# Running decay sums of a Mamba layer: from broadcasting products on TensorE to a write to memory and four loads back

## The chip, the cores and the metric

The kernel runs on one core of a Trainium2 chip. The core has TensorE (PE: matrix products, with its weight loads as a track of their own, PEld), VectorE (DVE), ScalarE (ACT), GpSimd (POOL) and SyncE (SP, which here issues the transfers). Each engine works through its own row of instructions in order and waits on semaphores for the others. The on-chip memory has 128 partitions; products land in PSUM banks. The metric is the device time of one execution in microseconds (us), the median of several. A profiled execution gives busy times, waits and the clock that TensorE was granted (1.00 is full speed).

## The reference

Two layers of a decoder trunk run on 256 tokens of width 1024, in float32. The first is a hybrid attention mixer with a dense SwiGLU, the second a Mamba-2 mixer with a layer of eight experts. The change concerns the Mamba mixer alone. Cut to what matters:

```python
z, xbc, dt = split_cols(h @ w_in, SSM_SPLITS)
...                                                # causal convolution, silu
dt = softplus(dt + dt_bias); A = -exp(a_log)       # 32 heads
a = (dt * A)...
cum = jnp.cumsum(a, axis=-1)                       # running decay sums per head and chunk
seg = cum[..., :, None] - cum[..., None, :]
L = jnp.exp(jnp.where(causal, seg, -jnp.inf))
cb = jnp.einsum('bclgn,bcsgn->bgcls', Cc, Bc)
y_diag = jnp.einsum('bgcls,bgrcls,bcsgrp->bclgrp', cb, L, xdt)
decay_from_start = jnp.exp(cum)
...                                                # states across chunks, y_off
y = (y_diag + y_off) + d_skip[:, None] * x
y = y * silu(z)
y = rmsnorm(y, per group) * norm_w
return y @ w_out
```

There are 32 heads of width 64 in four groups of eight, a state of 128, and `w_in` has 5152 columns and `w_out` 2048 rows.

## The kernel before

Weights come from memory in blocks of 1 MB, which SyncE loads into a ring of buffers ("raw": nine during the Mamba stage, sixteen once that stage's pools are freed). For the products of full accuracy each half of a block is split: ScalarE casts it to its high part (`wh`, L252), VectorE subtracts that to get the low part (`wl`, L253), and four buffers of each are in turn. A product is then three (L267 high by high, L268 and L269 high by low both ways). The half of an input block is 24 such products of 256 columns.

The Mamba stage has these parts. First dt is projected and its softplus taken; a scan (L968) gives `cum`, the running decay sums, 32 heads on 32 partitions by 256 tokens, in chunks of 128. `s_proj` runs for each of the four groups through five input blocks (20 in all): the first three go through the convolution (L986 on ScalarE, three steps L988 on VectorE) into `xbc`, the last two give z, whose silu is `zs` (L1021), in a single buffer. `s_core` runs for each group (core 0 to 3 below): C times B (L1031, L1032), transposes of x (L1042) scaled into `xd` (L1044), and then four pairs of heads, j = 0 to 3. For a pair it needs the sums of two heads on all 128 partitions: `cums(j)` gets them with two products that pick a head's row (L1052, `pick` with `chl`, the sums split in high and low parts) into the PSUM bank "pb". ScalarE takes from there the four differences (L1066, relu into `seg`, two buffers), the decay from the start (L1069, exponential into `fo`) and the exponential of seg (L1070); VectorE multiplies by C times B (L1073, L1075); TensorE makes six products (L1080 to L1082, twelve instructions in the trace), and VectorE adds x (L1083) and multiplies by `zs` (L1085). A core ends with the norm of its group: the square of y (L1088), sums over partitions (L1091), `ms` (L1093), a product (L1096), a reciprocal square root on both engines (L338 to L342), and y scaled (L1101). `outs` splits y (L1115 cast, L1116 low part `yl`) and runs the output projection with 512-column products. When the stage is over, the expert weights follow to the end (L1313).

An order by hand, `SSM_ORDER`, writes the steps out (p: a step of `s_proj`, c: of `s_core`, m and t: of the next part's preparation; the output projection's are drained last). A scheduler then sets each engine's row from that, from what depends on what and from when it takes an engine to be free, so that a step taken away can shift others in the rows.

ScalarE's functions come in tables; a change from one set to another (silu, or exp with square root's) is an ACT_TABLE_LOAD.

Of the kernel before, what the change touches and what calls it, by code (L numbers as in the profile page):

```python
# [8 lines left out]
F32 = mybir.dt.float32  # L9
BF16 = mybir.dt.bfloat16  # L10
F32R = mybir.dt.float32r
# [5 lines left out]
D, T, KD = 1024, 256, 8  # L17
# [168 lines left out]
def trunk_kernel(ctx: ExitStack, tc: tile.TileContext, d: dict, out: bass.AP):  # L186
    nc = tc.nc
    V, S, G, PE = nc.vector, nc.scalar, nc.gpsimd, nc.tensor
# [8 lines left out]
    def pbank(tag):  # L197
        return ps_p.tile([128, 512], F32, name=tag, bufs=4 if tag == "pa" else 2)
# [12 lines left out]
    def P(n):  # L211
        s, w = _PC[n]
        return pc[:, s:s + w]

    def K(n):
        s, w = _CS[n]
        return cs[:, s:s + w]
# [6 lines left out]
    def ring(which):  # L224

        pools = raws if which == "raw" else hls
        i = turn[which] % sum(n for _, n in pools)
        turn[which] += 1
        for p, n in pools:
            if i < n:  # L230
                return p
            i -= n

    def load(ap):

        ap = ap.rearrange("p a b c -> p (a b c)") if len(ap.shape) == 4 else ap.rearrange("p a b -> p (a b)")
        r = ring("raw").tile([128, 2048], F32, name="raw")
        nc.sync.dma_start(r[:, :ap.shape[1]], ap)
        return r[:, :ap.shape[1]]
# [131 lines left out]
    def hpair():  # L371
        return (act_p.tile([128, KD, T], F32R, name="hh"), act_p.tile([128, KD, T], F32R, name="hl"))
# [31 lines left out]
    def norm_h(m, dg):  # L404
        A, B = mod_cols(m)
        h = hpair()
        norm_T(dg, lambda k, ps: split_act(h[0][:, k], h[1][:, k], ps, A[:, k:k + 1], B[:, k:k + 1], k % 2))
        return h
# [86 lines left out]
    h = hpair()  # L495
    with ExitStack() as hx:
# [245 lines left out]
        def all_values():  # L742
            for r in range(4):
                pos_.append(pbank("pa"))
                values(prs[r], pos_[r])
                yield

        def finish():
            for r in range(4):
                PE.matmul(pos_[r][:, :T], vcb[:, r], cpT, start=False, stop=True, skip_group_check=True)  # L750
                split_act(mb[0][:, r], mb[1][:, r], pos_[r][:, :T])
                yield
# [112 lines left out]
        def mods():  # L865
            for c in (4, 5):
                mod_load("hyb", 2 * c, 2 * c + 2)
                yield
            mod_gate("hyb", gate)
            yield  # L870
            for c in range(4):
                if c in (0, 3):
                    mod_load("dense", 2 * c, 2 * c + 2)
                else:
                    mod_sum(*mod_part("dense", c, hw.tile([128, 512], F32, name="at", bufs=1)))
                yield

        def consts():
# [6 lines left out]
                     V=all_values(), F=finish(), g=gla(), m=mods(), o=out_nsa())  # L885
# [19 lines left out]
    h = norm_h("dense", dgs)  # L905
# [46 lines left out]
    h = norm_h("ssm", dgs)  # L952
    with ExitStack() as sx:
        sy = sx.enter_context(tc.tile_pool(name="ssmy", bufs=3))
        sp = sx.enter_context(tc.tile_pool(name="ssm", bufs=1))
# [11 lines left out]
        cum = sw.tile([32, T], F32, name="fo")  # L967
        V.tensor_tensor_scan(cum, resets(sw, 32, T, 128, "seg"), dx_, 0.0, op0=OP.mult, op1=OP.add)  # L968

        chl = sp.tile([64, T], F32R, name="chl")  # L970
        S.copy(chl[:32], cum)
        V.tensor_sub(chl[32:], cum, chl[:32].bitcast(F32))
        pick = sp.tile([64, 32], F32R, name="pick")
        S.copy(pick, K("sel32")[:64])
        dtd = sw.tile([32, 128], F32, name="ms", bufs=1)
        act(dtd, cum[:, :128], AF.Exp, bias=cum[:, 127:128], scale=-1.0)
        V.tensor_mul(dtd, dtd, dtv[:, :128])
# [49 lines left out]
        def s_core(g):  # L1027
            xbc, zs = xz[g]
            bT, cT, xT = xbc[:, 0], xbc[:, 1], xbc[:, 2:]
            pcb = pbank("pc")  # L1030
            PE.matmul(pcb[:, :T], bT[:, :128], cT, start=True, stop=True)  # L1031
            PE.matmul(pcb[:, T:T + 128], bT[:, 128:], cT[:, 128:], start=True, stop=True)  # L1032
            cbm = sw.tile([128, 3, 128], F32, name="cbm", bufs=1)
            V.tensor_mul(cbm[:, 0], pcb[:, :128], tri)
            V.tensor_mul(cbm[:, 1], pcb[:, T:T + 128], tri)
            S.copy(cbm[:, 2], pcb[:, 128:T])
            xd = sw.tile([128, 3, 512], F32, name="xd", bufs=1)

            def x_tok(c):
                px = pbank("pc")  # L1040
                for j in range(4):
                    PE.transpose(px[:, j * 128:(j + 1) * 128], xT[:, j, c * 128:(c + 1) * 128], ident)  # L1042
                for o_, i in ((c, c),) + (((2, 4),) if c == 0 else ()):
                    V.tensor_mul(xd[:, o_].rearrange("p (h n) -> p h n", h=8),  # L1044
                                 px.rearrange("p (h n) -> p h n", h=8),
                                 tk[:, i, 8 * g:8 * g + 8, None].to_broadcast([128, 8, 64]))

            def cums(j):
                pcu = pbank("pb")
                for e in range(2):  # L1050
                    hh = 8 * g + 2 * j + e
                    PE.matmul(pcu[:, e * T:(e + 1) * T], pick[:, hh:hh + 1].to_broadcast([64, 128]), chl,  # L1052
                              start=True, stop=True)
                return pcu

            y = xT
            pcu = cums(0)
            x_tok(0)
            x_tok(1)
            yield  # L1060
            for j in range(4):
                h0 = 8 * g + 2 * j
                sg = sw.tile([128, 2, 2, 128], F32, name="seg")
                for e in range(2):
                    for c in range(2):
                        act(sg[:, e, c], pcu[:, e * T + c * 128:e * T + (c + 1) * 128], AF.Relu,  # L1066
                            bias=tk[:, 2 + c, h0 + e:h0 + e + 1], scale=-1.0)
                fo = sw.tile([128, 2, 128], F32, name="fo")
                act(fo, pcu.rearrange("p (e n) -> p e n", e=2)[:, :, 128:], AF.Exp)  # L1069
                act(sg, sg, AF.Exp, scale=-1.0)  # L1070
                if j < 3:
                    pcu = cums(j + 1)
                V.tensor_mul(sg.rearrange("p e c n -> p e (c n)"), sg.rearrange("p e c n -> p e (c n)"),  # L1073
                             cbm[:, 0:2].rearrange("p c n -> p (c n)")[:, None, :].to_broadcast([128, 2, 256]))
                V.tensor_mul(fo, fo, cbm[:, 2:3].to_broadcast([128, 2, 128]))  # L1075
                yield
                py = pbank("pc")
                for e in range(2):
                    o_, cc = slice(64 * e, 64 * e + 64), slice(128 * j + 64 * e, 128 * j + 64 * e + 64)
                    PE.matmul(py[o_, :128], xd[:, 0, cc], sg[:, e, 0], start=True, stop=True)  # L1080
                    PE.matmul(py[o_, 128:T], xd[:, 1, cc], sg[:, e, 1], start=True, stop=False)
                    PE.matmul(py[o_, 128:T], xd[:, 2, cc], fo[:, e], start=False, stop=True)  # L1082
                V.scalar_tensor_tensor(y[:, j], xT[:, j], P("dsk")[:, 4 * g + j:4 * g + j + 1], py[:, :T],  # L1083
                                       op0=OP.mult, op1=OP.add)
                V.tensor_mul(y[:, j], y[:, j], zs[:, j])  # L1085
                yield
            yt = sy.tile([128, 4, T], F32, name="y") if g < 3 else sw.tile([128, 4, T], F32, name="zs", bufs=1)
            act(yt, y, AF.Square)  # L1088
            pms = pbank("pc")
            for j in range(4):  # L1090
                PE.matmul(pms[32 * j:32 * j + 32, :T], K("ones")[:, :32], yt[:, j], start=True, stop=True)  # L1091
            ms = sw.tile([128, T], F32, name="ms", bufs=1)
            S.copy(ms, pms[:, :T])  # L1093
            yield
            pms = pbank("pc")
            PE.matmul(pms[:, :T], K("sel32")[:, :1].to_broadcast([128, 128]), ms, start=True, stop=True)  # L1096
            V.tensor_scalar(ms, pms[:, :T], 1.0 / 512, EPS, op0=OP.mult, op1=OP.add)
            ry = rsqrt_(ms, [128, T], sw, ("sq", "sq"))
            yield
            for j in range(4):  # L1100
                V.scalar_tensor_tensor(yt[:, j], y[:, j], P("sgn")[:, 4 * g + j:4 * g + j + 1], ry,  # L1101
                                       op0=OP.mult, op1=OP.mult)
            ys.append(yt)
            yield
# [84 lines left out]
    with ExitStack() as mx:  # L1189
# [342 lines left out]
        with tc.If(nmax > 0):  # L1532
# [3 lines left out]
            for h_ in range(2):  # L1536
                ps = pbank("pc")
                for q in range(4):
                    k = 4 * h_ + q
                    PE.matmul(ps[:, q * 128:(q + 1) * 128], macc["moe"][:, 16 + k:17 + k].to_broadcast([128, 128]),  # L1540
                              ident, start=True, stop=True)
                S.copy(gate[:, h_ * 512:(h_ + 1) * 512], ps)
            with tc.For_i(0, NE, 1) as e:
                for base in (0, 128):
# [23 lines left out]
                    for f0 in range(0, FE, 512):  # L1568
                        c, h_ = divmod(f0, 1024)
                        pgu = [pbank("pa") for _ in range(2)]  # L1570
                        for k in range(KD):
# [7 lines left out]
                            for u in range(2):  # L1579
                                PE.matmul(pgu[u].rearrange("p (j n) -> p j n", n=rk_.shape[3]), g2[:, k], rk_[:, u],  # L1580
                                          start=k == 0, stop=k == KD - 1)
# [11 lines left out]
                        for f in range(4):  # L1593
                            if f % 2 == 0:
                                r = load(d["e_dn"][bass.ds(e, 1), f0 // 256 + f // 2].rearrange("a p k n -> p a k n"))
                            for n in range(2):
                                PE.matmul(py[n], at[:, f * 128:(f + 1) * 128],
                                          r[:, (f % 2) * D + n * 512:(f % 2) * D + n * 512 + 512],
                                          start=f0 == 0 and f == 0, stop=f0 == FE - 512 and f == 3)
# [28 lines left out]
```

## Time and profile before

| what | value |
|---|---|
| median of 3 runs | 1454.12 us (1453.21 to 1457.64) |
| profiled execution | 1455.68 us, span 1453.7 us |
| busy: TensorE, VectorE, ScalarE | 1412.4, 562.8, 435.8 us |
| transfers | 493.66 MB, mean 340 GB/s |
| stages | hybrid to about 240 us, dense to 375, Mamba to 595, experts to the end |

Busy times count what an engine executes; a row of TensorE that is full says that it is not waiting, not that it is at its peak. In a timeline, the space from one start to the next is what an instruction costs in its row, and its duration can overlap the next one's.

### The profile page before, as it was taken

Reading aid. Unit: us, or ns where it says so; the run is one execution under the profiler, and the core shown is the slowest. Engines: PE = TensorE matmul, PEld = TensorE weight load, DVE = VectorE, ACT = ScalarE, POOL = GpSimd, SP = SyncE. Lnnn points to the kernel's source line nnn. Section 1 sums busy time; section 2 is a strip of 40 time slices with the busy share of each in tenths; the row PEclk is TensorE's granted clock in tenths of the full one; section 3 lists DMA queues with packets and bytes.
Section 4 is the critical chain, followed back from the end, with each engine's and each line's share of the span. In section 5 each row is a group of like instructions: output and inputs, shape, how many; then the busy total and the mean of one; then the engine's idle time right before and its main releaser. Section 6 shows DMA issues by size and latency. Waiting matters only on the chain.

```text
span 1453.7 us, 28564 instructions
## 1 busy us (share of the span) xinstructions
PE 1412.4 (97%) x12249; PEld 803.0 (55%) x12249; DVE 562.8 (39%) x1098; ACT 435.8 (30%) x854; POOL 5.3 (0%) x13
## 2 busy tenths in 40 slices
PE   6999999999999999999999999999999999999995
PEld 6866699999799987633433333333334333333331
DVE  7888588875678778510110111010100100100102
ACT  5577554444577685210100001000001000000001
POOL 0000000000000000000000000000000000000000
PEclk9999999999999999999999999999999999999998
DMA  9876778976544434799999999999999999999994
GB/s 382 351 271 251 297 295 334 375 300 241 232 146 154 165 117 144 286 397 363 350 413 420 420 420 420 417 421 420 420 420 419 420 421 420 420 419 420 420 420 163
DMA packets 68964, 493.66 MB, mean 340 GB/s; under 512 B 7648, under 2 KB 7904, under 8 KB 9568
## 3 DMA queue, kind: packets, MB, share of 16 engines
q1 hardware_dynamic: 68832, 491.77, 84.4%
q8 instruction: 98, 1.61, 0.4%
q14 instruction: 34, 0.28, 0.0%
HBM read 490.70 MB, written 1.05 MB: 338 GB/s over the span
## 4 chain that ended last, share of the span: by engine, by line
PE 93%; ACT 2%; DMA 2%; DVE 2%; issue 0%; SPq 0%; ACTq 0%; DVEq 0%
PE pa L1313 33%; PE pb L1313 16%; PE pa L267 7%; PE pa L268 7%; PE pa L269 7%; PE pb L268 3%; PE pb L269 3%; PE pb L267 3%; PE pc L1385 2%; PE pc L1347 1%; PE pc L1271 1%; DMA raw<-in_e_dn_dram 1%; ACT wh L252 1%; PE pb L702 1%; DMA raw<-in_hyb_mod_dram 1%; PE pa L732 1%
## 5 line engine op out<-in xcount | busy, mean ns | idle before, releaser
L1313 PE MATMUL pa<-raw,gx 128*32 128x512 f32 (+1 forms) x5120 | 506.4, 540 | 0.0
L1313 PEld LDWEIGHTS pa<-raw,gx 128*32 128x32 f32 x5120 | 167.2, 110 | 299.5 <-issue 261.3
L1313 PE MATMUL pb<-raw,at 128*32 128x512 f32 x2240 | 253.0, 594 | 2.2 <-DMA raw<-in_e_dn_dram 2.2
L1481 DVE TENSOR_TENSOR sg<-sg,pa 128x256 f32<-128x256 f32 (+1 forms) x80 | 31.0, 387 | 474.4 <-ACT sg L1480 472.7
L253 DVE TENSOR_TENSOR wl<-raw,wh 128x1024 fp32r<-128x1024 f32 (+1 forms) x155 | 185.4, 1204 | 57.2 <-ACT wh L252 57.0
L252 ACT CAST wh<-raw 128x1024 fp32r<-128x1024 f32 (+1 forms) x155 | 159.0, 1036 | 121.9 <-PE pb L268 53.0
L1313 PEld LDWEIGHTS pb<-raw,at 128*32 128x32 f32 x2240 | 70.5, 110 | 154.1 <-issue 144.8
L1480 ACT ACTIVATE sg<-pa 128x256 f32<-128x256 f32 (+1 forms) x80 | 28.5, 357 | 346.4 <-PE pa L1313 346.4
L267 PE MATMUL pa<-hh,wh 128*128 128x256 f32 (+1 forms) x392 | 112.4, 289 | 1.6 <-ACT wh L252 0.7
L268 PE MATMUL pa<-hl,wh 128*128 128x256 f32 (+1 forms) x392 | 111.4, 285 | 0.8 <-DVE hl L386 0.8
L269 PE MATMUL pa<-hh,wl 128*128 128x256 f32 (+1 forms) x392 | 111.3, 285 | 0.0
L267 PE MATMUL pb<-hh,wh 128*128 128x256 f32 (+1 forms) x360 | 101.8, 284 | 1.9 <-ACT hh L380 1.9
L268 PE MATMUL pb<-hl,wh 128*128 128x256 f32 (+1 forms) x360 | 102.3, 284 | 0.0
L269 PE MATMUL pb<-hh,wl 128*128 128x256 f32 (+1 forms) x360 | 102.2, 284 | 0.0
L1348 ACT COPY at<-pc 128x512 f32<-128x512 f32 (+2 forms) x32 | 17.4, 545 | 262.4 <-PE pb L1313 134.9
L281 DVE SCALAR_TENSOR_TENSOR junk<-raw,scb 128x1024 bf16<-128x1024 f32 x72 | 87.8, 1219 | 1.6 <-DMA raw<-in_hyb_mod_dram 1.0
L267 PEld LDWEIGHTS pa<-hh,wh 128*128 128x128 f32 (+1 forms) x392 | 73.8, 189 | 5.5 <-ACT wh L252 1.7
L268 PEld LDWEIGHTS pa<-hl,wh 128*128 128x128 f32 (+1 forms) x392 | 74.2, 189 | 2.1 <-DVE hl L386 0.9
L269 PEld LDWEIGHTS pa<-hh,wl 128*128 128x128 f32 (+1 forms) x392 | 74.1, 189 | 0.8 <-DVE gu L629 0.3
L267 PEld LDWEIGHTS pb<-hh,wh 128*128 128x128 f32 (+1 forms) x360 | 68.4, 190 | 2.9 <-ACT hh L380 2.1
L268 PEld LDWEIGHTS pb<-hl,wh 128*128 128x128 f32 (+1 forms) x360 | 68.6, 191 | 1.0 <-DVE hl L386 0.5
L269 PEld LDWEIGHTS pb<-hh,wl 128*128 128x128 f32 (+1 forms) x360 | 68.6, 191 | 0.3
(424 smaller groups left out, 1466.1 us busy)
## 6 DMA issues: line engine op xcount, KB each, us to landing
raw<-in_e_gu_dram SPq DMA_DIRECT2D x192, 1024.0 KB, 18.5
raw<-in_e_dn_dram SPq DMA_DIRECT2D x112, 1024.0 KB, 19.7
raw<-in_e_gl_dram SPq DMA_DIRECT2D x32, 1024.0 KB, 18.3
raw<-in_d_gu_dram SPq DMA_DIRECT2D x22, 1024.0 KB, 7.3
raw<-in_s_in_dram SPq DMA_DIRECT2D x20, 1024.0 KB, 4.8
raw<-in_hyb_mod_dram SPq DMA_DIRECT2D x12, 1024.0 KB, 9.6
raw<-in_ssm_mod_dram SPq DMA_DIRECT2D x12, 1024.0 KB, 7.1
raw<-in_d_dn_dram SPq DMA_DIRECT2D x11, 1024.0 KB, 7.9
```

The lines of the kernel that those rows point to most:

```text
L252: hi_last[0] = S.copy(hi[:, :n], r)
L253: lo_last[0] = V.tensor_sub(lo[:, :n], r, hi[:, :n].bitcast(F32))
L267: PE.matmul(ps, a[0], b[0], start=start, stop=False, **kw)
L268: PE.matmul(ps, a[0], b[1], start=False, stop=False, **kw)
L269: return PE.matmul(ps, a[1], b[0], start=False, stop=stop, **kw)
L281: V.scalar_tensor_tensor(jk, r[:, q * D:(q + 1) * D], 1.0, scb, op0=OP.mult, op1=OP.mult, accum_out=macc[m][:, 2 * j + q:2 * j + q + 1])
L702: PE.matmul(pss[g], qbT[g * 64:(g + 1) * 64, r, q * 128:(q + 1) * 128], kT[g * 64:(g + 1) * 64, :, :n], start=True, stop=True)
L1313: up_last[0] = PE.matmul(ps[32 * j:32 * j + 32, :rhs.shape[1]], lhs, rhs, start=start, stop=stop)
L1348: (V.tensor_copy if i else S.copy)(at[:, i:i + n].rearrange("p a n -> p (a n)"), pt_[:, :n * 128])
L1385: PE.matmul(pso[b], at_place[e, q][:, h, b], p[:, q], start=i == 0, stop=i == 2 * n - 1)
L1480: last = act(sg[:, r, :w], pg[r][:, :w], AF.Silu)
L1481: V.tensor_mul(sg[:, r, :w], sg[:, r, :w], pg[r][:, w:2 * w])
```

## The change

The sums in high and low parts and the table that picks a head are gone, and so are the 32 products. Instead ScalarE's queue writes `cum` (32 x 256 floats, 32 KB) to a buffer in memory, and at the start of each core SyncE's queue loads the eight heads of its group, 2048 floats in one row, to all 128 partitions at once: one block of 1 MB in the ring of weight buffers. The relus and exponentials read their two heads from there. The order by hand is as it was.

```diff
--- before.py
+++ after.py
@@ -967,11 +967,8 @@
         cum = sw.tile([32, T], F32, name="fo")
         V.tensor_tensor_scan(cum, resets(sw, 32, T, 128, "seg"), dx_, 0.0, op0=OP.mult, op1=OP.add)
 
-        chl = sp.tile([64, T], F32R, name="chl")
-        S.copy(chl[:32], cum)
-        V.tensor_sub(chl[32:], cum, chl[:32].bitcast(F32))
-        pick = sp.tile([64, 32], F32R, name="pick")
-        S.copy(pick, K("sel32")[:64])
+        dr = sx.enter_context(tc.tile_pool(name="dr", bufs=1, space=bass.MemoryType.DRAM)).tile([32, T], F32, name="dr")
+        S.dma_start(dr, cum)
         dtd = sw.tile([32, 128], F32, name="ms", bufs=1)
         act(dtd, cum[:, :128], AF.Exp, bias=cum[:, 127:128], scale=-1.0)
         V.tensor_mul(dtd, dtd, dtv[:, :128])
@@ -1045,13 +1042,10 @@
                                  px.rearrange("p (h n) -> p h n", h=8),
                                  tk[:, i, 8 * g:8 * g + 8, None].to_broadcast([128, 8, 64]))
 
+            cb = load(dr[8 * g:8 * g + 8].rearrange("h n -> (h n)")[None, :].to_broadcast([128, 8 * T])[:, None, :])
+
             def cums(j):
-                pcu = pbank("pb")
-                for e in range(2):
-                    hh = 8 * g + 2 * j + e
-                    PE.matmul(pcu[:, e * T:(e + 1) * T], pick[:, hh:hh + 1].to_broadcast([64, 128]), chl,
-                              start=True, stop=True)
-                return pcu
+                return cb[:, 2 * j * T:2 * (j + 1) * T]
 
             y = xT
             pcu = cums(0)
```

Line numbers of the kernel after are 3 lower from L974 on, and 6 lower behind L1052 (L1080 is L1074, L1115 is L1109).

The rows of the engines move with it. On TensorE, before, at the last product of the input projection (L269 with `hh`, `wl`) and what stands behind it, unit j = 3 of core 2, a pair of sums for core 3 and the first products of the output projection (`wh`, `hh`):

```order
L268 MATMUL pa<-hl,wh 128x256
L269 MATMUL pa<-hh,wl 128x256
L1080 MATMUL pc<-seg,xd 64x128
L1081 MATMUL pc<-seg,xd 64x128
L1082 MATMUL pc<-fo,xd 64x128
L1080 MATMUL pc<-seg,xd 64x128
L1081 MATMUL pc<-seg,xd 64x128
L1082 MATMUL pc<-fo,xd 64x128
L1052 MATMUL pb<-chl,pick 128x256 x2
L267 MATMUL pa<-wh,hh 128x512
```

Now the same place holds core 2's units j = 2 and 3 (the end of the second is shown), then the four sums of squares of its norm, the norm, C times B and the transposes of core 3, and only then the output projection:

```order
L1076 MATMUL pc<-fo,xd 64x128
L1074 MATMUL pc<-seg,xd 64x128
L1075 MATMUL pc<-seg,xd 64x128
L1076 MATMUL pc<-fo,xd 64x128
L1085 MATMUL pc<-y,cs 32x256 x4
L1090 MATMUL pc<-ms,cs 128x256
L1028 MATMUL pc<-xbc 128x256
L1029 MATMUL pc<-xbc 128x128
L1039 MATMUL pc<-cs,xbc 128x128 x4
L267 MATMUL pa<-wh,hh 128x512
L268 MATMUL pa<-wl,hh 128x512
```

What moved: no product of the output projection stands between the last input block and core 2's norm any more.

On ScalarE, before, in the same place, the cast of y of core 0 (L1115) and the relus of a pair of core 3 stand ahead of the silu of z (L1021) and the square of core 2's y (L1088):

```order
L252 CAST wh<-raw 128x1024 x2
L1115 CAST hh<-y 128x1024
L1066 ACTIVATE seg<-pb,tk 128x128 x4
L1069 ACTIVATE fo<-pb 128x256
L1070 ACTIVATE seg<-seg 128x512
L252 CAST wh<-raw 128x1024
L1021 ACT_TABLE_LOAD
L1021 ACTIVATE zs<-pa 128x512 x2
L348 ACT_TABLE_LOAD
L1088 ACTIVATE y<-xbc 128x1024
L1115 CAST hh<-y 128x1024
L1093 COPY ms<-pc 128x256
```

Now (the four relus of core 3's first pair stand right ahead):

```order
L1063 ACT_TABLE_LOAD
L1063 ACTIVATE fo<-raw 128x256
L1018 ACT_TABLE_LOAD
L1018 ACTIVATE zs<-pa 128x512 x2
L348 ACT_TABLE_LOAD
L1082 ACTIVATE y<-xbc 128x1024
L1064 ACTIVATE seg<-seg 128x512
L1060 ACTIVATE seg<-raw,tk 128x128 x4
L1087 COPY ms<-pc 128x256
L1063 ACTIVATE fo<-raw 128x256
L1064 ACTIVATE seg<-seg 128x512
L1109 CAST hh<-y 128x1024
```

What moved: the cast of y of core 0 stands behind the silu, the square and the copy of `ms`, and there is a table load on each side of fo.

On VectorE, before, from the norm of core 1 (L1101) to the next split of weights, with the convolution of core 3's input:

```order
L1101 SCALAR_TENSOR_TENSOR y<-xbc,pc,sq 128x256 x4
L1044 TENSOR_TENSOR xd<-pc,tk 128x512
L988 SCALAR_TENSOR_TENSOR xbc<-pa,pc,xbc 128x255
L1073 TENSOR_TENSOR seg<-seg,cbm 128x512
L988 SCALAR_TENSOR_TENSOR xbc<-pa,pc,xbc 128x254
L1075 TENSOR_TENSOR fo<-fo,cbm 128x256
L988 SCALAR_TENSOR_TENSOR xbc<-pa,pc,xbc 128x253
L988 SCALAR_TENSOR_TENSOR xbc<-pa,pc,xbc 128x255
L253 TENSOR_TENSOR wl<-raw,wh 128x1024
```

Now the end of the same stretch, from the second fo behind that norm to the next split:

```order
L1069 TENSOR_TENSOR fo<-fo,cbm 128x256
L985 SCALAR_TENSOR_TENSOR xbc<-pa,pc,xbc 128x255 x2
L985 SCALAR_TENSOR_TENSOR xbc<-pa,pc,xbc 128x254 x2
L985 SCALAR_TENSOR_TENSOR xbc<-pa,pc,xbc 128x253 x2
L1077 SCALAR_TENSOR_TENSOR xbc<-xbc,pc 128x256
L985 SCALAR_TENSOR_TENSOR xbc<-pa,pc,xbc 128x255 x3
L985 SCALAR_TENSOR_TENSOR xbc<-pa,pc,xbc 128x254 x2
L985 SCALAR_TENSOR_TENSOR xbc<-pa,pc,xbc 128x253 x2
L985 SCALAR_TENSOR_TENSOR xbc<-pa,pc,xbc 128x254
L1079 TENSOR_TENSOR xbc<-xbc,zs 128x256
L985 SCALAR_TENSOR_TENSOR xbc<-pa,pc,xbc 128x253
L253 TENSOR_TENSOR wl<-raw,wh 128x1024
```

What moved: the split that stood behind four convolution steps stands behind fifteen.

## Rows read from the trace of the kernel before

**Rows 1.** Three stretches: length, busy us (instructions) of each engine, PEclk, DMA, GB/s:

```profile
400.00:595.00 195.00, 194.45 (x1438) 174.16 (x1436) 150.42 (x266) 134.43 (x231) 0.00 (x0) 1.00 0.40 141
640.00:740.00 100.00, 100.00 (x1075) 37.70 (x1071) 9.42 (x30) 10.85 (x28) 0.00 (x0) 1.00 0.96 367
740.00:1425.00 685.00, 676.66 (x6595) 241.00 (x6587) 73.27 (x162) 59.70 (x139) 0.00 (x0) 1.00 1.01 420
```

**Rows 2.** Timeline of TensorE: start, duration, engine, line, operation, tiles, shape, count, [idle before]:

```profile
403.15 0.36 PE L267 MATMUL pa<-hh,wh 128*128 128x256 f32 x1 [0.25 <-DVE xbc L988]
...
478.68 0.28 PE L268 MATMUL pa<-hl,wh 128*128 128x256 f32 x1
478.80 0.28 PE L269 MATMUL pa<-hh,wl 128*128 128x256 f32 x1
479.01 0.50 PE L1052 MATMUL pb<-chl,pick 64*128 64x256 f32 x2
479.44 0.43 PE L1080 MATMUL pc<-seg,xd 128*64 128x128 f32 x2
...
480.51 0.50 PE L1052 MATMUL pb<-chl,pick 64*128 64x256 f32 x2
```

**Rows 3.** Landing time of the broadcast load of a 4 KB row, line 944:

```profile
DMA to landing us min/median/max: 4.6/4.6/4.6
```

**Rows 4.** The page's DMA issues: tiles, queue, count, KB each, us to landing:

```profile
raw<-in_e_gu_dram SPq DMA_DIRECT2D x192, 1024.0 KB, 18.5
```

**Rows 5.** Timeline of VectorE, after the scan and ahead of the convolutions:

```profile
396.41 0.68 DVE L968 TENSOR_TENSOR_SCAN fo<-seg,sq 32x256 f32<-32x256 bf16 x1
...
503.42 1.21 DVE L253 TENSOR_TENSOR wl<-raw,wh 128x1024 fp32r<-128x1024 f32 x1
...
505.62 0.68 DVE L1044 TENSOR_TENSOR xd<-pc,tk 128x512 f32<-128x512 f32 x1
506.22 0.41 DVE L342 SCALAR_TENSOR_TENSOR sq<-sq 128x256 f32<-128x256 f32 x1
...
507.16 1.66 DVE L1101 SCALAR_TENSOR_TENSOR y<-xbc,pc,sq 128x256 f32<-128x256 f32 x4
...
510.45 0.47 DVE L988 SCALAR_TENSOR_TENSOR xbc<-pa,pc,xbc 128x254 f32<-128x254 f32 x1
510.84 0.41 DVE L1075 TENSOR_TENSOR fo<-fo,cbm 128x256 f32<-128x256 f32 x1
...
511.95 1.21 DVE L253 TENSOR_TENSOR wl<-raw,wh 128x1024 fp32r<-128x1024 f32 x1
```

**Rows 6.** Timeline of ScalarE, at the first sums and at the tail of core 2:

```profile
404.52 1.17 ACT L1066 ACTIVATE seg<-pb,tk 128x128 f32<-128x128 f32 x4
...
406.31 1.10 ACT L252 CAST wh<-raw 128x1024 fp32r<-128x1024 f32 x1
...
527.64 1.14 ACT L1066 ACTIVATE seg<-pb,tk 128x128 f32<-128x128 f32 x4
528.80 1.28 ACT L1069 ACT_TABLE_LOAD   x1
530.09 0.39 ACT L1069 ACTIVATE fo<-pb 128x256 f32<-128x256 f32 x1
530.37 0.62 ACT L1070 ACTIVATE seg<-seg 128x512 f32<-128x512 f32 x1
...
533.88 1.04 ACT L1115 CAST hh<-y 128x1024 fp32r<-128x1024 f32 x1 [1.01 <-PE pa L269]
...
539.01 1.09 ACT L1021 ACTIVATE zs<-pa 128x512 f32<-128x512 f32 x2
...
543.31 0.36 ACT L1093 COPY ms<-pc 128x256 f32<-128x256 f32 x1
```

**Rows 7.** Stretches of the first layer in which the granted clock fell:

```profile
82.00:87.00 5.00, 3.03 (x12) 1.33 (x12) 3.98 (x14) 4.89 (x14) 0.00 (x0) 1.00 1.02 429
87.00:91.00 4.00, 4.00 (x35) 1.59 (x34) 4.00 (x8) 2.51 (x8) 0.00 (x0) 0.57 1.07 397
```

## The prediction

> **What bounds the kernel now.** I read the stretches first: between 400 and 595 us, the Mamba stage around the change, TensorE is busy 194.45 of 195 us at the full granted clock, while VectorE is busy 150, ScalarE 134 and the DMA engines 0.40 of the time [rows 1]. The stage is TensorE's, and what is taken out of its row, or put into it as idle time, is what moves. The same view tells how a shift there reaches the end: from 640 to 740 us TensorE is still busy the whole time and the transfers run at 367 GB/s, because they wait for it; from 740 on they run at 420 GB/s with nothing left over [rows 1]. In both stretches the expert weights come through a ring of buffers that is full, so a shift of the stage's end shifts the kernel's end one for one, in either direction.
>
> Then the timeline of TensorE: a pair of L1052 products takes 0.43 us, from its start at 479.01 to the next product at 479.44, and the twelve L1080 to L1082 instructions of one head pair (a unit, below) take 1.07 us, to 480.51 [rows 2]. Plain products of 256 columns start 0.12 us apart (478.68, 478.80) [rows 2].
>
> **What the change takes away.** There are 16 pairs: 16 x 0.43 = 6.9 us of TensorE's row. At 403.15, right behind the first pairs, TensorE waits 0.25 us for a convolution result [rows 2]; there a removed pair only makes the wait longer, so I count 6.6 us. The cast and subtraction that split the decay sums (L971, L972) and the cast of the selection table (L974) lie beside TensorE's work, and I count nothing for them.
>
> **What it adds on the transfers.** One write of 32 KB from ScalarE's queue and four loads of 1 MB in SyncE's queue, each in a slot of the nine-slot ring. 4 MB in a stage whose DMA engines are busy 0.40 of the time costs nothing by itself, and of the nine slots one is held by the sums at a time. The trace has no write like it and no load that repeats one row of 8 KB over 128 partitions. The nearest row is a load that repeats a 4 KB row, 512 KB, in 4.6 us [rows 3]; the far one is a block of the expert weights in the crowded stretch, 18.5 us [rows 4]. With 4.6 us each for write and load, from the scan's end at 397.1 (396.41 + 0.68) [rows 5], the first sums are there at 406.3. ScalarE wants them at 404.52, and the cast behind them stood at 406.31 [rows 6]; so that cast comes about 2 us later. Three halves of weights cast ahead, of 24 products each, are 3 x 24 x 0.12 = 8.6 us of work for TensorE, which covers that. Below nothing it can't go, since nobody waited for the sums before. I take 0, by the nearest row; the far one is a rival below. What is queued behind that load on SyncE (further blocks of the input projection) has its cover in the blocks already in the ring. For the write only a page has a price: the Trainium skill (DMA: Bandwidth & Descriptors, Latency and other measured facts) speaks of about 2 us of fixed cost, most of it the receipt from memory; as an estimate by it the first sums would land at 403.7 us, and the sum below stays as it is. No run here shows that yet.
>
> **What it moves.** With fewer products in the row, all of the input projection comes ahead of the second half of core 2 (the third group of heads), and the first products of the output projection come behind that core's norm. Two places pay.
>
> First, VectorE ahead of the last blocks of the input projection. In the row of before, 9.7 us lie from the start of one low-part split (503.42) to the end of the next (511.95 + 1.21) [rows 5], with four convolution steps between them, and TensorE doesn't wait. In the changed row the stretch between two such splits holds three xd products and two of seg at 0.60 each, three steps of the square root, two of fo and two of y at 0.41, the four of y's norm in 1.66 and fifteen convolution steps at 0.39 [rows 5]: 3.0 + 2.9 + 1.7 + 5.9 = 13.5 us, and the two splits at its ends 2.4, together 15.9. TensorE's row holds in the same time 73 products of the input projection, 73 x 0.12 = 8.8, two units, 2.1, and eight transposes, at most 1.0: 11.9 us. Then it wants the split that stands behind the convolution steps. Ends: 0 (if TensorE comes late to that place itself, as it did before) and 4.0, the whole difference; durations overlap a little in such a row, so I take 3.5.
>
> Second, the tail of core 2. In TensorE's row behind the last product of the input projection stand only units j = 2 and 3 (2.1 us), four sums of squares, the norm, C times B and the transposes, and then the output projection. In the row of before its products stand between them, and the cast of y that they need is done early (533.88) [rows 6]. In the changed row of ScalarE that cast stands behind the whole tail. The chain there, from the last product: 0.9 for unit 2, whose seg buffer the next relus reuse; four relus 1.14; a table load 1.28; fo 0.28; a table load 1.28; the two zs 1.09; a table load 1.28; the square of y, as wide as the cast, 1.04 [rows 6]. That is 8.3 us, of which TensorE fills 2.1: 6.2 idle. Then the exponential (0.62), four relus (1.14) and the copy of ms (0.36) [rows 6], 2.1 us, of which the four sums fill 4 x 0.12: 1.6 idle. Then fo, exponential and cast, 0.28 + 0.62 + 1.04 = 1.9, against seven products (0.9) and a VectorE step (0.41) between them: 0.6 idle. Last the low part of y, 1.2 by the split of the same width, against three products of 512 columns (0.7): 0.5 idle. Together 8.9 us. Lower end 2.7 (only the last three waits stay, if relus and tables come early), upper end 10.
>
> **TensorE's clock.** From 82 to 87 us TensorE was busy 3.03 of 5 us at the full clock, and in the next 4 us, with work all the time, the granted clock was 0.57, so mostly the lower of its two levels, 1.2 GHz [rows 7]. That lost 4 x 0.43 = 1.7 us. Both places make stretches with more idle time than that. Ends 0 and 3.4; I take 0.7, since the low clock can also fall on time that is idle anyway. The Trainium skill (TensorE: Matmul & The Clock Gate, Why this matters for your kernels) has a rule that speaks against this change: no idle gaps between bursts of matmuls, or the array goes back to 1.2 GHz; the trace agrees, with its 0.57. By that rule the tail would pay its 1.7 us for certain, and the kernel would take 1461.6 us.
>
> **Sum.** -6.6 + 0 + 3.5 + 8.9 + 0.7 = +6.5 us. On the profiled execution, 1455.68 us (its span of 1453.7 and 2 us around it), that makes 1462.2; this execution stands 1.6 above the median of the runs, 1454.12, and on the median the forecast is 1460.6 us.
>
> **Rivals.**
> Faster: the whole 6.6 us reach the end, 1447.5 us. The mechanism: at the tail of core 2 ScalarE runs ahead, and the relus and tables are done while TensorE is still in its last block. For it: ScalarE is busy only 134 of 195 us [rows 1]. Against it: those relus need the seg buffer that unit 2 still reads, and that unit stands behind the last block. It decides from the point where both places idle less than 6.6 us together.
> About the same: the first place costs nothing and the tail's 8.9 us come without a fall of the clock: +2.3, 1456.4 us. For it: before, TensorE bore 9.7 us between two splits without waiting [rows 5]. Against it: 15.9 is half as much again.
> Slower still: both places at their upper ends, each with a fall of the clock: -6.6 + 4.0 + 8.9 + 3.4 = +9.7, 1463.8 us. For it: the 0.57 [rows 7].
> The transfers don't do what they should: 128 reads of the same 8 KB are as slow as a block in the crowded stretch, 18.5 us [rows 4]. Then the first sums come at 397.1 + 4.6 + 18.5 = 420.2, ScalarE stands with its casts behind them, TensorE runs out of split weights at about 415 and gets the next at 424: 9 us more than the forecast, 1470 us. Against it: this stretch is not crowded.
>
> **How the numbers follow.** Forecast 0.45, about the same 0.30, faster 0.12, slower still 0.08, slow transfers 0.05. 0.3% of the median is 4.4 us, about what a measurement of this kernel can tell from no change. Of the forecast's 0.45 some 0.06 fall under 4.4 us (the first place at 1 us or below). So slower 0.39 + 0.08 + 0.05 = 0.52, within 0.3% 0.36, faster 0.12. The likeliest case alone spans 1456.5 to 1464; the range reaches down into the upper part of the faster case and up past the third rival, but not to the fourth: 1449 to 1466.
>
> **What would show it.** Right: no L1052 and some 6.6 us less work in TensorE's row; waits of TensorE for wl (L253) or xbc ahead of the last input blocks of 1 to 4 us; behind the last input product, waits for the square of y, for ms and for the cast of y that sum to about 9 us; a granted clock under 1 there; the first expert products 5 to 7 us later. Wrong: TensorE's waits in the Mamba stage staying under 4 us (then the same or faster), or a wait of ScalarE of more than 5 us for a load of the sums (then the fourth rival).

## The result and the profile after

The changed kernel takes 1468.27 us (median of 5, 1462.43 to 1472.46), the kernel before 1457.64 us (median of 5, 1453.21 to 1459.69): a ratio of 1.0077, 95% interval 1.0056 to 1.0098, some 11 us slower. The forecast was 1460.6 us, a range of 1449 to 1466, and 6.5 us slower. So the direction and both places were right, the size was short, and the time lies above the range. The profiled execution of after is the fastest of its five (1462.43 us, span 1460.5).

The three stretches of [rows 1], in the same view of after:

```profile
400.00:595.00 195.00, 183.27 (x1350) 166.91 (x1351) 144.31 (x249) 134.84 (x224) 0.00 (x0) 0.96 0.51 183
640.00:740.00 100.00, 100.00 (x1075) 37.72 (x1071) 8.58 (x28) 10.11 (x26) 0.00 (x0) 1.00 0.95 367
740.00:1425.00 685.00, 677.06 (x6577) 240.33 (x6570) 73.57 (x162) 58.74 (x138) 0.00 (x0) 1.00 1.01 420
```

The Mamba stage is no longer full: TensorE stands still for 11.7 of 195 us and has 0.96 of its clock, where it had 0.6 us and 1.00. The experts' stretches are unchanged. What TensorE waits for from 372 to 612 us (line waited at, releaser, us in total, times, longest): before has two in the stage,

```profile
PE pa L267 <- ACT wh L252: 0.3, 1, 0.3
PE pa L267 <- DVE xbc L988: 0.3, 1, 0.3
```

and after has

```profile
PE pc L1085 <- ACT y L1082: 7.0, 1, 7.0
PE pa L267 <- DVE xbc L985: 2.8, 2, 1.6
PE pa L269 <- DVE wl L253: 2.1, 1, 2.1
PE pc L1090 <- ACT ms L1087: 0.9, 1, 0.9
```

These are the two places of the forecast, and one more wait of 1.2 us for xbc at 400, where before waited 0.25 [rows 2]. The timeline of TensorE shows them, and what comes behind the first and the longest:

```profile
397.20 1.84 PE L321 MATMUL pc<-cs,part 128*128 128x1 f32 x16
400.24 0.36 PE L267 MATMUL pa<-hh,wh 128*128 128x256 f32 x1 [1.20 <-DVE xbc L985]
...
402.10 0.41 PE L268 MATMUL pa<-hl,wh 128*128 128x256 f32 x1
402.31 0.41 PE L269 MATMUL pa<-hh,wl 128*128 128x256 f32 x1
...
514.92 0.35 PE L267 MATMUL pa<-hh,wh 128*128 128x256 f32 x1 [1.59 <-DVE xbc L985]
...
517.47 0.47 PE L269 MATMUL pa<-hh,wl 128*128 128x256 f32 x1 [2.07 <-DVE wl L253]
...
538.95 1.08 PE L1085 MATMUL pc<-y,cs 128*32 128x256 f32 x8 [6.96 <-ACT y L1082]
540.89 1.22 PE L1090 MATMUL pc<-ms,cs 128*128 128x256 f32 x2 [0.86 <-ACT ms L1087]
541.90 1.06 PE L1028 MATMUL pc<-xbc 128*128 128x256 f32 x2
542.76 0.63 PE L1029 MATMUL pc<-xbc 128*128 128x128 f32 x2
543.18 1.06 PE L1039 MATMUL pc<-cs,xbc 128*128 128x128 f32 x4
543.90 0.78 PE L267 MATMUL pa<-wh,hh 128*128 128x512 f32 x1
```

From 540.89 to 543.90 nothing waits, and yet a few small products take 3.0 us. In the timeline of before the same norm and C times B take 1.00 us, from 543.97 to the next product at 544.97; here they take 2.29 (540.89 to 543.18):

```profile
543.97 0.59 PE L1096 MATMUL pc<-ms,cs 128*128 128x256 f32 x2
...
544.97 0.48 PE L268 MATMUL pa<-wl,hh 128*128 128x512 f32 x1
```

The granted clock says why. Stretches of after in the form of [rows 7]:

```profile
402.00:404.00 2.00, 2.00 (x11) 2.00 (x11) 2.00 (x5) 1.74 (x6) 0.00 (x0) 0.50 1.01 422
518.00:520.00 2.00, 2.00 (x11) 2.00 (x11) 2.00 (x5) 0.00 (x0) 0.00 (x0) 0.50 0.84 352
534.00:538.00 4.00, 0.00 (x0) 0.00 (x0) 0.17 (x1) 3.97 (x6) 0.00 (x0) 0.59 0.74 256
538.00:546.00 8.00, 6.19 (x26) 4.54 (x27) 3.73 (x8) 6.55 (x14) 0.00 (x0) 0.57 0.00 0
```

The clock falls to 1.2 GHz in three places: at 402, behind sixteen products of one column each and the wait of 1.2 us; at 518, behind 1.6 and 2.1 us; and in the long wait itself, from about 534.7 to 545, and in some 5 us of that TensorE works. The transfers, against [rows 3, 4] (the page's form, a median for the four loads):

```profile
raw<-dr SPq DMA_DIRECT2D x4, 1024.0 KB, 4.7
...
dr<-fo ACTq DMA_DIRECT2D x1, 32.0 KB, 1.5
```

They cost as little as assumed: 4.7 us for a broadcast load (the median of four; the second took 10.3), 1.5 us for the write. That is less than the 2 us that the Trainium skill speaks of (DMA: Bandwidth & Descriptors, Latency and other measured facts). ScalarE waits for none of the loads; its first relus on them start right behind its casts:

```profile
398.79 2.96 ACT L252 CAST wh<-raw 128x1024 fp32r<-128x1024 f32 x3
401.62 1.29 ACT L1060 ACTIVATE seg<-raw,tk 128x128 f32<-128x128 f32 x4
```

To compare executions I use the length of the Mamba stage from the scan to the first expert product. The run's other part varies by falls of the clock in the first layer, which the change doesn't touch: before lost 5.1 us of full clock there (18 to 24, 86 to 92 and 100 to 106 us) and after's profiled execution none; its scan starts 2.9 us earlier. Before goes from 396.41 [rows 5] to

```profile
604.89 0.64 PE L1313 MATMUL pa<-raw,gx 128*32 128x512 f32 x4
```

which is 208.5 us; after (VectorE's and TensorE's timelines) takes 217.4 us, 8.9 more:

```profile
393.48 0.68 DVE L968 TENSOR_TENSOR_SCAN fo<-seg,sq 32x256 f32<-32x256 bf16 x1
...
610.86 0.64 PE L1307 MATMUL pa<-raw,gx 128*32 128x512 f32 x4
```

### The profile page after: what moved, and what is told of

Its sections match the earlier page's. It is cut to its first block, busy times and chain, and to the rows that moved or that the text cites. A ratio compares the mean times of both kernels' runs of the same rounds, so it can differ in the third digit from the quotient of the medians.

```text
span 1460.5 us, 28513 instructions
## 1 busy us (share of the span) xinstructions
PE 1406.8 (96%) x12217; PEld 800.6 (55%) x12217; DVE 562.6 (39%) x1097; ACT 440.6 (30%) x854; POOL 5.3 (0%) x13
## 4 chain that ended last, share of the span: by engine, by line
PE 87%; DMA 5%; DVE 3%; ACT 3%; issue 1%; SPq 0%; ACTq 0%
PE pa L1307 31%; PE pb L1307 15%; PE pa L267 7%; PE pa L268 7%; PE pa L269 7%; PE pb L268 3%; PE pb L269 3%; PE pb L267 3%; DMA raw<-in_e_dn_dram 2%; PE pc L1379 2%; PE pc L1265 1%; DMA raw<-in_e_gl_dram 1%; DMA raw<-in_e_gu_dram 1%; PE pc L1341 1%; PE pb L400 1%
## 5 line engine op out<-in xcount | busy, mean ns | idle before, releaser
L269 PE MATMUL pa<-hh,wl 128*128 128x256 f32 (+1 forms) x392 | 112.3, 288 | 2.1 <-DVE wl L253 2.1
L269 PE MATMUL pb<-hh,wl 128*128 128x256 f32 (+1 forms) x360 | 101.8, 283 | 0.0
L269 PEld LDWEIGHTS pa<-hh,wl 128*128 128x128 f32 (+1 forms) x392 | 75.3, 193 | 2.8 <-DVE wl L253 2.3
L269 PEld LDWEIGHTS pb<-hh,wl 128*128 128x128 f32 (+1 forms) x360 | 68.3, 190 | 0.1
```

What stands on the lines that cost most here:

```text
L269: return PE.matmul(ps, a[1], b[0], start=False, stop=stop, **kw)
```

## The experiments

The theory was that the change pays by the order of the rows, which leaves TensorE idle in two places, and by the clock that falls there. The main rival was that the transfers cost. Ratios are to the kernel before in the same runs, with a 95% interval. A difference between two ratios is uncertain by some 3 to 5 us; the length of the stage is that of one profiled execution.

**loads_added.** Transport added to before, whose products stay in use; the order of the rows is before's.

```diff
+        dr = ...; S.dma_start(dr, cum)
...
+            cb = load(dr[8 * g:8 * g + 8]...)
+            V.tensor_copy(sp.tile([128, 8], F32, name="cbx", bufs=1), cb[:, :8])
```

> The kernel before, with the write to memory and the four loads added: the products (L1052) stay and are used, each load is read once by a small copy on VectorE; TensorE's row keeps the order of before. Theory (the order of the rows costs): within 1.5 us of before, no new wait of TensorE over 1 us. Rival (the transfers cost, by slots of the ring, by ScalarE's queue or by their traffic): since the change gives back 6.6 us of products and still ends 11 us later, the transfers would cost 12 us or more, and TensorE would wait for split weights.

Measured 1.0011 (0.9998 to 1.0024), 1458.56 us; the stage takes 208.5 us, as before:

```profile
396.72 0.68 DVE L968 TENSOR_TENSOR_SCAN fo<-seg,sq 32x256 f32<-32x256 bf16 x1
...
605.19 0.64 PE L1318 MATMUL pa<-raw,gx 128*32 128x512 f32 x4
```

TensorE's waits are those of before. The transport is free in the stage, and the rival, which wanted 12 us, falls.

**products_kept.** The changed kernel, with the 32 products made for nobody.

```diff
             def cums(j):
+                pcu = pbank("pb")
+                for e in range(2):
+                    PE.matmul(pcu[...], pick[...], chl, ...)
                 return cb[:, 2 * j * T:2 * (j + 1) * T]
```

> The changed kernel, in which TensorE still makes the 32 products, whose results nobody reads. ScalarE's and VectorE's rows and the rest of TensorE's are those of the changed kernel. Theory (the order costs): both waits stay (about 7 and 5 us), and the products are on top as far as they don't fall into a wait: 3 to 7 us slower than the changed kernel, 13 to 18 us slower than before. Rival (the gain of the products was never there, they were hidden): the same as the changed kernel within 2 us.

Measured 1.0105 (1.0088 to 1.0123), 1473.80 us: by the ratios 4 us slower than the changed kernel, uncertain by 4, and 15 slower than before. The stage takes 223.4 us (399.12 to 622.56), 6.1 more than after's. The waits of the two places are those of after (7.0, 2.1, 1.6 and 0.9 us); the wait of 1.2 us at 400 is gone:

```profile
PE pc L1095 <- ACT y L1092: 7.0, 1, 7.0
PE pa L269 <- DVE wl L253: 2.1, 1, 2.1
...
404.99 5.13 PE L1056 MATMUL pb<-chl,pick 64*128 64x256 f32 x27
```

So the products cost time where nothing hides them, and the waits eat what their absence saves. By how much is not measured here, for nobody reads them and 27 of the 32 stand in one block (404.99 to 410.05), in part at half clock. And the tail's row is that of the changed kernel, with its wait, although all 32 are still made, ahead of it: less work in TensorE's row, the reason that the prediction gave, isn't needed to move the rest.

**no_transport.** The changed kernel without write and loads; the decay sums are replaced by stretches of the residual, so what follows works on other numbers, and the experts' stage can't be compared (5021 us in all). Only the Mamba stage is read.

```diff
             def cums(j):
-                return cb[:, 2 * j * T:2 * (j + 1) * T]
+                return x[:, j % 2, 256 * (j // 2):256 * (j // 2) + 2 * T]
```

> The changed kernel without the write and the four loads: the relus and exponentials read a tile that lies on the chip (two stretches of the residual), so the decay sums are left out and the numbers that follow are others. The order of the rows is that of the changed kernel. Theory (the order costs): as slow as the changed kernel within 2 us, 8 to 12 us slower than before, with the waits of 7.0 us for the square of y and 2 us for a split. Rival (the transfers cost): 6.6 us faster than before, without these waits.

In whole times the expectation can't be tested. In the stage:

```profile
PE pc L1081 <- ACT y L1078: 7.0, 1, 7.0
PE pa L269 <- DVE wl L253: 3.4, 2, 2.1
```

Both places are there without any transfer. The stage takes 220.9 us (398.08 to 618.93), 3.5 more than after's: new are waits of 1.4 and 1.3 us for the first split weights and a longer stretch at half clock behind them (406 to 413), and the wait of 1.2 us is gone. So the long waits need no transport, and by products_kept they come with the products made or not. What after, products_kept and no_transport share, and before and loads_added don't, is that ScalarE's relus no longer read a product of TensorE. That this is what lets the scheduler move the rows fits all five; how it comes to its order is not shown.

**order_new.** The changed kernel with another order by hand (the middle and the end of the list).

```diff
-SSM_ORDER = "... p c p c c c c c p c p c p c c p c c p c c c c c c c c t c ..."
+SSM_ORDER = "... p c c c p c c c p c p c p c c p c c p c c c o o o o c c c c c t c ..."
```

> The changed kernel with another order by hand: one input block of core 2 comes two steps later, and four steps of the output projection are written behind the last input block, so that its products stand again between that block and core 2's norm. Theory (the order costs): the waits for the square of y and for the split go, TensorE waits under 5 us from 375 to 610 us and its clock stays at 1.00 there, so the saving of 6.6 us comes out: 4 to 8 us faster than before, 13 to 19 faster than the changed kernel. Rival (the transfers cost): still slower than before by 8 us or more.

Measured 0.9967 (0.9952 to 0.9982), 1453.72 us: 4.8 us faster than before and 16 faster than the changed kernel. The stage takes 203.6 us (399.25 to 602.89), 4.8 less than before; its largest waits behind the scan are

```profile
PE pa L267 <- DVE xbc L985: 1.2, 1, 1.2
PE pc L1146 <- DVE br L1144: 1.1, 1, 1.1
```

One detail of the expectation failed: the clock fell once in the stage, at 406 to 411 us, behind the 1.2 us, and once ahead of it, at 382 to 387.

**tail_only.** The four steps of the output projection alone (o in the list) are brought forward; the first place stays.

```diff
+SSM_ORDER = "... p c p c p c c p c c p c c c o o o o c c c c c t c ..."
```

> The changed kernel with four steps of the output projection written behind the last input block, and nothing else moved: TensorE has products of the output projection in the tail of core 2 again; the first place (the split behind fifteen convolution steps) stays as it is. Theory (both places cost, the tail the most): the wait of 7.0 us for the square of y goes, the waits for xbc and wl (1.6 and 2.1 us) stay with a fall of the clock behind them: 7 to 11 us faster than the changed kernel, within 0 to 4 us slower than before. Rival (the first place, with the falls of the clock that it sets off, is the main price): at most 4 us faster than the changed kernel.

Measured 1.0012 (1.0001 to 1.0024), 1458.53 us: 9.5 us faster than the changed kernel, as the theory said (7 to 11). The stage takes 210.4 us (395.05 to 605.45), 7.0 less than after's. The wait for the square of y is gone, the first place is there, and the low part of y is late:

```profile
PE pa L267 <- DVE xbc L985: 2.8, 2, 1.6
PE pa L269 <- DVE wl L253: 2.1, 1, 2.1
PE pa L269 <- DVE yl L1110: 1.5, 1, 1.5
```

So the rival (at most 4 us) falls. From here to order_new it is 6.5 us more by the ratios (1.0012 to 0.9967) and 6.8 by the stage; part of that is the wait of 1.5 us for yl, which only this run has. So the tail costs some 7 us or more, and the first place, with the clock behind it, some 5 to 7; that the tail is the larger price is likely, but the intervals don't show it.

**before_new_order.** Before, with order_new's list.

> The kernel before, products and all, with the order by hand of the run order_new. Theory: TensorE hardly waits in the Mamba stage of before (2.1 us from 372 to 606), so another order has nothing to give: within 2 us of before, and order_new's gain is the products'. Rival (the new order is better by itself and the change adds nothing): 4 to 6 us faster than before, as order_new.

Measured 0.9992 (0.9980 to 1.0003), 1455.11 us: the order alone gives nothing that can be told from none. By the ratios order_new lies 3.6 us under it, and by the stage 4.0 (207.6 us here, 393.64 to 601.24): order_new's gain needs the products gone. This run shows one thing more. Its rows around 400 us are those of before, with before's wait of 0.25 us, and yet the clock fell there:

```profile
402.00:404.00 2.00, 2.00 (x11) 2.00 (x11) 2.00 (x4) 1.73 (x6) 0.00 (x0) 0.50 0.00 0
```

**fill_wait, fill_more and fill_even.** Products that nobody needs, in the changed kernel's long wait; fill_even also has the step t one place earlier in the order by hand.

```diff
             pms = pbank("pc")
+            if g == 2:
+                for q in range(20):                       # fill_wait: 24, and none below
+                    PE.matmul(pms[:, :T], h[0][:, 0, :128], h[0][:, 0, :T], start=True, stop=True)
+                for q in range(6):
+                    PE.matmul(pms[:, :T], ident, xz[3][1][:, q % 4], start=True, stop=True)
```

> The changed kernel with 24 products that nobody needs (256 columns, 0.12 us each) in TensorE's row right ahead of the sums of squares of core 2; no other row changes. They shorten the idle time there from 7.0 to about 4.1 us and must not lengthen the chain, which is ScalarE's. Theory (idle time costs twice, once as a wait and once by the clock that falls behind it): the low clock behind the tail gets shorter, 0.5 to 2.5 us faster than the changed kernel. Rival (the wait alone costs): the same as the changed kernel within 0.5 us.

Measured 1.0069 (1.0047 to 1.0091), 1467.80 us: not to be told from the changed kernel, and the interval is too wide to tell theory from rival. The stage takes 217.4 us (397.97 to 615.41), as after's; there the theory's gain is missing, as the rival said. The wait fell to 3.9 us, but the clock fell all the same, only later, and TensorE worked about as long at the low clock:

```profile
542.00:550.00 8.00, 5.73 (x23) 4.21 (x24) 3.27 (x7) 6.99 (x15) 0.00 (x0) 0.57 0.00 0
```

> As fill_wait, with 20 such products at once and 6 more, in full accuracy, that wait for the silu of z (zs): of the 7.0 us no idle stretch over about 1.5 us is left. The rows behind move: a product for the router now stands where it waits for VectorE, about 2.5 us by the durations of the rows. Theory (idle time costs by the clock as well): the clock stays at 1.00 from 530 to 550 us, which gives back the 2 to 3 us that were lost at half speed, so the time is that of the changed kernel within 1.5 us in spite of the new wait. Rival (the wait alone costs): 2 to 3 us slower than the changed kernel.

Measured 1.0090 (1.0070 to 1.0110), 1471.70 us, by the ratios 2 us slower than the changed kernel, with intervals that overlap; the stage takes 222.1 us (399.31 to 621.36), 4.7 more than after's. By the stage the theory's time failed. But the run doesn't decide for the rival either: the clock did stay up through the tail, and fell behind the new wait of 2.7 us for the router instead:

```profile
530.00:550.00 20.00, 16.90 (x131) 14.58 (x130) 10.15 (x18) 17.30 (x28) 0.00 (x0) 1.00 0.44 158
553.00:561.00 8.00, 6.74 (x34) 5.80 (x35) 5.95 (x13) 5.71 (x15) 0.00 (x0) 0.57 0.01 3
```

> As fill_more, with the router's step one place earlier in the order by hand, so that no wait of over 1.5 us should be left from the tail of core 2 on; the first place (1.6 and 2.1 us) stays. Without any effect of the clock the moved rows cost about 2 us, by the waits that they add. Theory (idle time costs by the clock as well): no fall of the clock from 525 to 560 us, which gives back the 2.5 us or so that the changed kernel loses there at half clock, so the time is that of the changed kernel within 1.5 us, and 2 to 5 us under fill_more. Rival (the wait alone costs): 2 us or more slower than the changed kernel.

Measured 1.0065 (1.0041 to 1.0088), 1467.14 us, the time of the changed kernel and 3.6 us under fill_more; the stage takes 218.7 us (396.40 to 615.06), 1.3 more than after's. No wait of the tail is over 1.6 us, and the clock stays up; it also stayed up behind the wait of 1.2 us (1.19 here, to 403.17), where after's fell:

```profile
404.00:406.00 2.00, 2.00 (x20) 2.00 (x18) 2.00 (x6) 2.00 (x6) 0.00 (x0) 1.00 1.02 426
...
525.00:560.00 35.00, 29.74 (x219) 24.51 (x218) 23.55 (x44) 25.47 (x45) 0.00 (x0) 1.00 0.35 122
```

That is what the theory expected, but the intervals of these three overlap. So it is shown that filling keeps the clock up in the tail, and not how many us that gives back.

**after_again.** The changed kernel, executed and profiled once more.

> The changed kernel once more, for the rows of an execution other than its fastest (1462.4 us at a mean clock of 0.989; the median of its five was 1468.3 at 0.983). Theory (its price is the waits, the same in every execution, and falls of the clock, which vary): the same waits of TensorE within 0.2 us (7.0, 2.1, 1.6, 1.2), and more or longer stretches at half clock, also outside the Mamba stage. Rival (the waits themselves vary, by the transfers): other waits in the slower execution, or one of ScalarE for the loads of the sums.

1466.64 us at a mean clock of 0.985. The waits are the same (7.0, 2.8, 2.1, 0.9), the stage takes 217.2 us (396.75 to 613.99), and of the 4.2 us more than in the first profile 3.3 come ahead of it, where the clock fell at 18, 86 and 380 us as well, and 1.1 behind it. The five times of the changed kernel, 10 us apart, go with the mean clock: 1462.43 us at 0.989, 1472.46 at 0.981.

## Why the prediction was wrong, and where it was right

The stage's 8.9 us, by the forecast's own terms:

| term | forecast | measured in the profile |
|---|---|---|
| products | -6.6 | -7.0, and -0.9 for changes of form (below) |
| transfers | 0 | 0 (loads_added) |
| waits: first place, tail, the rest | 3.5 + 8.9 | 3.7 + 7.8 + 1.2, less 0.6 that before had: +12.1 |
| clock | 0.7 | about +5, an estimate from the spacing of products (below) |
| sum | +6.5 | about +9; the stage grew by 8.9 |

The step that failed is the term for the clock: "I take 0.7, since the low clock can also fall on time that is idle anyway". It did fall on idle time, from 534.7 to 539, but it lasted beyond, and it fell three times. At 402.10 and 402.31 two plain products of after start 0.21 us apart, where they stood 0.12 [rows 2]; behind each of the first two waits some 16 such products cost about 1.5 us, and in the tail the small products of 540.89 to 543.90 and those around them more than 2. So the price of one fall, 1.7, was about right, and the number of falls and the length of the last were not. The upper end, 3.4, was too low as well, for it counted two falls. The fall at 402 can't be put down to the change alone: before_new_order has it without the longer wait, and fill_even has the wait without it. The last two waits of the tail that I had counted (0.6 and 0.5 us) are missing from the profile, since the slowed products cover them; in fill_even, where the clock stays up, waits for the cast and the low part of y are there, 0.3 and 0.8 us.

The range failed by this and by its base. I carried the sum to a median of three runs, 1454.12; in later runs before stood at 1456.4 to 1457.6. With 8.9 us on 1457.1 the time would be 1466.0, and the measured interval (8 to 14 us) holds that; the rest of the 11 us, if there is one, stays open. That the profiled execution, at 1462.43 us, meets the 1462.2 of the sum, and that its first expert products come 6.0 us later (604.89 to 610.86), inside the 5 to 7 of the sign, is luck: its first layer had no falls of the clock and gave back 2.9 us of the 8.9.

The saving was sized right: 16 pairs are 7.0 us in the timeline, though more of it went into the wait at 403 than the 0.3 that was counted (0.25 grew to 1.2). The first place's wait, 3.7 us in two parts, came as worked out from the row of VectorE (3.5): its two splits and what lies between take 15.6 us, where the sum had 15.9. And the tail's came as from ScalarE's chain (6.2 and 1.6, measured 7.0 and 0.9), with its three table loads:

```profile
501.82 1.22 DVE L253 TENSOR_TENSOR wl<-raw,wh 128x1024 fp32r<-128x1024 f32 x1
...
516.19 1.22 DVE L253 TENSOR_TENSOR wl<-raw,wh 128x1024 fp32r<-128x1024 f32 x1
...
531.15 1.28 ACT L1060 ACTIVATE seg<-raw,tk 128x128 f32<-128x128 f32 x4
532.44 1.28 ACT L1063 ACT_TABLE_LOAD   x1
...
534.16 1.28 ACT L1018 ACT_TABLE_LOAD   x1
...
536.54 1.28 ACT L348 ACT_TABLE_LOAD   x1
537.84 1.06 ACT L1082 ACTIVATE y<-xbc 128x1024 f32<-128x1024 f32 x1
```

One reason of the prediction doesn't hold: "With fewer products in the row" the rest was to move, and products_kept has the same tail with all the products still made. The rule of the Trainium skill that I weighed (TensorE: Matmul & The Clock Gate, Why this matters for your kernels) had the better price, 1461.6 us, and was still short: it was counted for the tail alone, and here the clock also fell at 402 and behind waits of 1.6 and 2.1 us with work between them. Of the rivals, "slower still", at 1463.8 us and with a chance of 0.08, came nearest in its mechanism: both places with a fall of the clock each. In its number the slow transfers, 1470 us, came nearer, but that is chance, for no load was waited for.

## What to carry to other kernels

Work taken from the engine that sets the pace is worth its time only if the rows stay as dense as they were: where a scheduler orders them, read what now stands ahead of each wait, and mend the order together with the change; here that turned 11 us lost into 4.8 us won. Look also for what a moved instruction no longer has to wait for, and not only for what was taken away. Price an idle stretch of TensorE at its wait and at the slow clock behind it, once for each such stretch, and give a short one a chance and not a certainty. Carry a sum to a base of many runs.

## What the runs showed of the hardware

A 1 MB load that repeats one row of 8 KB over 128 partitions lands in 4.7 us, no slower than a block of weights (5.0 in the same execution; both are medians, and one of the four loads took 10.3), and a write of 32 KB from ScalarE's queue in 1.5 us. Behind the waits of 1.6 and 2.1 us the clock fell in all eight profiled executions that have both (in after, 0.50 from 518 to 520), and with the unfilled wait of 7.0 us in all four. Behind the wait of 1.2 us, ahead of which TensorE had sixteen products of one column, it fell in six of seven executions, and in the same place of the rows of before, with a wait of 0.25 us, in one of three (before_new_order). And a change of form costs: in the timeline of before the space behind a plain product and ahead of another form is longer than behind one of its own (478.80 to 479.01 is 0.21 us against 0.12 [rows 2]), summed over 46 such places of the stage about 2.8 us, and over 34 of after about 1.9 us.
